# An RWKV-7 and block attention trunk: the state's carry over a chunk as a product and a sum beside PE, with another order of the work

## The chip, the cores and the metric

The kernel runs on one core of a Trainium2 chip. Its engines are TensorE (PE; its weight loads are shown apart as PEld), VectorE (DVE), ScalarE (ACT), GpSimd (POOL) and SyncE (SP), which issues most transfers. Each engine works off its own list of instructions in the order of that list, and semaphores hold an instruction back until what it reads is there. The metric is the device time of one execution in microseconds (us), lower being better.

## The reference

There are 256 tokens of width 1024 and two layers. The first is RWKV-7 time mixing with 16 heads of 64; the second is block attention with one block of 256 keys, so that it comes to causal attention behind the shared keys and values. Cut to what matters here, with the recurrence that the change touches:

```python
# layer 1
r, wdn, k, v, adn, gp = [(h + xx * mu[i]) @ w_in[:, cols(i)] for i in range(6)]
decay = exp(-exp(-softplus(-(w0 + tanh(wdn) @ w2)) - 0.5))
a = sigmoid(a0 + adn @ a2)
kk = normalized per head (k * k_k);  k = k * (1 + (a - 1) * k_a);  b = kk * a
def step(S, inp):                       # S: 64 x 64 for each head, over 256 tokens
    sa = einsum('bhvk,bhk->bhv', S, kk_t)
    S = S * d_t - sa[..., None] * b_t + v_t[..., None] * k_t
    y = einsum('bhvk,bhk->bhv', S, r_t)
y = (group_norm(y) + bonus) * silu(gp);  x = x + y @ w_out_a
# between: K and V from rms_norm(x) @ w_kv, K with QK-norm and partial rotary
# layer 2
q, g = rms_norm(x) @ w_in_b;  o = softmax(q K^T / 8, causal) V
x = x + (o * silu(g)) @ w_out_b
```

All inputs and outputs are float32.

## The kernel before

**Dense products.** The work is set by products of 256 by 1024 activations with weights, in two blocks of 128 tokens (b = 0, 1) and column halves of 512 (n = 0, 1). Most run as three reduced float32 products for one full one: ACT rounds a weight tile `raw` to `whi`, DVE forms the rest `wlo` (tiles of 128 by 1024), and the activations `z` are split in the same manner into `zhi` and `zlo`. PE then accumulates `wlo x zhi`, `whi x zlo` and `whi x zhi` into the banks `acc`. For the one matrix named in `WHOLE` ("v") the full float32 product `raw x z` is taken with no splitting. `dense` spawns such a product in four quarters of its contraction; `mixed_split` makes the mixed activations of layer 1.

**The recurrence.** It runs in chunks of 64 tokens, c = 0 to 3, for each half n of the heads (8 heads, in pairs on the two halves of the partitions, q = 0, 1). Within a chunk the 64 steps are solved at once by an inverse made beforehand (`inverse`, whose small products read and write ZX, AD, AB, QS and Z). `recurrence(n, c)` takes the state and values of the chunk, a tile UV of 64 + 64 rows, through these steps: `UV x WL` on PE; a copy of it by DVE into `u`; `u x Z` on PE; its negative, U, written back into UV by DVE and ACT; and for c < 3 `UV x NBK` on PE, which is what the chunk adds to the state. Two DVE operations (q = 0, 1) then write the sum times the decay `eLT` into the state part of the next chunk's UV. The old state has to be in that sum. For c = 0 it is zero; for c = 1 and 2 `chunk_y` copies it into the PSUM bank `st` by a product with the identity (`ident`, a part of the tile `con`), from which on `UV x NBK` accumulates:

```python
(mm(st[own[q]].rearrange("p j k -> p (j k)"), ident[own[q], own[q]],
    t[own[q], q].rearrange("p j k -> p (j k)"), 0.255, start=True, stop=False, skip_group_check=True)
 for q in range(2))
```

So the bank `st` is taken at the start of the chunk and given back behind the two DVE operations. `chunk_y` also makes the chunk's output with `UV x RR`; `group_norm` follows it on ACT, DVE and POOL.

**The order.** It isn't the order of the source. A planner (the class `Weave`) runs when the program is built: each piece of work is a generator that yields operations with estimated costs, waits for events or takes buffers; whenever an engine is free by these estimates, the ready operation of least number in `PR` goes next. `SWITCH` adds to that number where ACT would have to load another function table, `STICK` where PE would go from wide products to small ones or back, `ALT` says when an operation that DVE or POOL may do (`vg`) goes to POOL, and `KEEP` and `WARM` set when PE's clock is to be kept up (in the latter with products of a zero tile). `ORDER_A` and `ORDER_B` list the columns of the two layers' projections in the order in which their weights are fetched. Buffers are handed out in the same manner: five of `u` (`N_U2`), three of `raw`, four PSUM banks `ps`. The result is one fixed list for each engine.

**Lines.** In the rows a helper's line stands for all its uses: L413 for a product, L417 for a transposition by the identity, L308 for an operation of DVE, ACT or POOL. The tile's names tell them apart.

## Time and profile before

| what | us |
|---|---|
| median of 3 runs (356.96 to 357.12) | 356.97 |
| the profiled execution's own time | 358.23 |
| its span, from the first to the last instruction | 356.4 |
| PE busy | 348.1 (98%) |
| DVE busy | 290.6 (82%) |
| ACT busy | 205.7 (58%) |
| POOL busy | 47.0 (13%) |

A row's busy time counts an instruction from its start to its modelled end; on PE the ends overlap the next start, so what a product costs PE is read from one start to the next. Where a row ends in a bracket, it is the idle time of that engine just ahead of it, with the engine that ended it.

### The profile page before, as it was taken

How to read it: one execution, taken by the hardware profiler on the slowest of the kernel's cores; microseconds unless marked ns; L12 is line 12 of the kernel's file. 1: busy time of each engine (PE TensorE's matmuls, PEld its weight loads, DVE VectorE, ACT ScalarE, POOL GpSimd, SP SyncE). 2: the span in 40 equal slices, each digit the busy share in tenths (PEclk: the TensorE clock that was granted, in tenths of full speed). 3: DMA queues.
4: the chain of work that ended last, by engine and by line, in shares of the span. 5: the costliest groups of instructions: out<-in, count | busy, mean ns of one | idle time of the engine just before them, and what ended most of it. 6: DMA issues, size and time to landing. Idle time of an engine off the chain costs nothing.

```text
span 356.4 us, 7161 instructions
## 1 busy us (share of the span) xinstructions
PE 348.1 (98%) x2782; PEld 273.0 (77%) x2782; DVE 290.6 (82%) x582; ACT 205.7 (58%) x405; POOL 47.0 (13%) x71
## 2 busy tenths in 40 slices
PE   6999999999899999999999999999999999999995
PEld 6995877878458786567777788898877788789884
DVE  1899799999998988996669989885679969697723
ACT  3519988762336573254846547556459964696620
POOL 1100032000130000201001261060504004000000
PEclk9999999999999999999999999999999999999999
DMA  7825463763173741245545431365550366313403
GB/s 219 231 53 190 136 204 122 211 166 106 26 252 119 181 127 28 80 139 175 208 140 181 155 124 64 133 224 200 177 205 4 120 243 221 128 60 121 157 21 118
DMA packets 29738, 51.40 MB, mean 144 GB/s; under 512 B 4412, under 2 KB 5764, under 8 KB 29704
## 3 DMA queue, kind: packets, MB, share of 16 engines
q1 hardware_dynamic: 29480, 50.85, 44.8%
q8 instruction: 22, 0.36, 0.4%
q10 hardware_dynamic: 224, 0.09, 0.1%
q14 instruction: 12, 0.10, 0.1%
HBM read 48.32 MB, written 1.05 MB: 139 GB/s over the span
## 4 chain that ended last, share of the span: by engine, by line
PE 91%; DVE 5%; DMA 1%; issue 1%; ACT 1%; ACTq 0%; DVEq 0%
PE acc L413 63%; PE ps L413 21%; PE ps L417 7%; DMA con<-in_consts_dram 1%; DVE zlo L308 1%; DVE u L308 1%; DVE WL L308 1%; DVE RR L308 1%; DVE wlo L308 0%; DVE XF L308 0%; DVE xw L308 0%; ACTq L495 0%; DVE AD L308 0%; DVE eL L308 0%; ACT u L308 0%
## 5 line engine op out<-in xcount | busy, mean ns | idle before, releaser
L308 DVE TENSOR_TENSOR wlo<-raw,whi 128x1024 fp32r<-128x1024 f32 x70 | 85.0, 1218 | 26.7 <-ACT whi L308 26.2
L308 ACT ACTIVATE whi<-raw 128x1024 fp32r<-128x1024 f32 x70 | 73.9, 1060 | 40.7 <-PE acc L413 20.0
L413 PE MATMUL acc<-wlo,zhi 128*128 128x512 f32 x120 | 51.2, 427 | 0.0
L413 PE MATMUL acc<-whi,zhi 128*128 128x512 f32 x120 | 47.1, 392 | 0.0
L413 PE MATMUL acc<-whi,zlo 128*128 128x512 f32 x120 | 47.0, 391 | 0.0
L413 PE MATMUL acc<-whi,z 128*128 128x512 f32 x128 | 39.8, 392 | 0.0
L413 PEld LDWEIGHTS acc<-whi,z 128*128 128x128 f32 x128 | 24.1, 188 | 4.8
L413 PEld LDWEIGHTS acc<-wlo,zhi 128*128 128x128 f32 x120 | 22.5, 188 | 6.0 <-issue 0.5
L413 PEld LDWEIGHTS acc<-whi,zhi 128*128 128x128 f32 x120 | 22.5, 188 | 5.1
L413 PE MATMUL acc<-wlo,z 128*128 128x512 f32 x64 | 26.3, 410 | 0.0
L413 PEld LDWEIGHTS acc<-whi,zlo 128*128 128x128 f32 x120 | 22.6, 188 | 4.1 <-issue 0.5
L413 PE MATMUL acc<-zb,whi 128*128 128x256 f32 x128 | 23.3, 282 | 0.0
L413 PE MATMUL acc<-whi,zb 128*128 128x512 f32 x64 | 20.1, 395 | 0.0
L413 PE MATMUL acc<-whi,zf 128*128 128x512 f32 x64 | 19.8, 390 | 0.0
L413 PEld LDWEIGHTS acc<-zb,whi 128*128 128x128 f32 x128 | 19.7, 189 | 0.1
L413 PE MATMUL acc<-zb,wlo 128*128 128x256 f32 x64 | 18.8, 294 | 0.0
L308 POOL TENSOR_TENSOR nrm<-nrm,half 128x8 f32<-128x8 f32 x4 | 8.7, 2174 | 76.3 <-DVE nrm L308 76.3
L308 ACT ACTIVATE zhi<-u 128x256 fp32r<-128x256 f32 (+1 forms) x16 | 7.9, 522 | 17.1 <-DVE u L308 13.2
L413 PE MATMUL acc<-raw,zhi 128*128 128x512 f32 x32 | 15.5, 612 | 1.5 <-ACT u L308 1.5
L413 PE MATMUL acc<-raw,zlo 128*128 128x512 f32 x32 | 16.3, 615 | 0.0
L308 POOL TENSOR_SCALAR vr<-vr 128x8 f32<-128x8 f32 x4 | 3.0, 756 | 91.8 <-DVE vr L308 91.8
L308 ACT ACTIVATE AB<-ps 32x256 f32<-32x256 f32 (+1 forms) x32 | 10.3, 321 | 7.1 <-PE ps L413 5.9
(219 smaller groups left out, 749.2 us busy)
## 6 DMA issues: line engine op xcount, KB each, us to landing
raw<-in_w_in_a_dram SPq DMA_DIRECT2D x32, 512.0 KB, 4.6
raw<-in_w_kv_dram SPq DMA_DIRECT2D x16, 512.0 KB, 4.1
raw<-in_w_in_b_dram SPq DMA_DIRECT2D x16, 512.0 KB, 3.6
raw<-in_w_out_a_dram SPq DMA_DIRECT2D x8, 512.0 KB, 3.7
raw<-in_w_out_b_dram SPq DMA_DIRECT2D x8, 512.0 KB, 3.4
x<-in_x_dram SPq DMA_DIRECT2D x8, 256.0 KB, 3.4
out_dram<-x SPq DMA_DIRECT2D x8, 128.0 KB, 1.9
NBK<-kkh SPq DMA_DIRECT2D x6, 128.0 KB, 6.0
```

Source lines behind the costliest of these rows:

```text
L308: op = Op(eng, us, lambda: getattr(obj, name)(*a, **k), table=table, banks=banks(*a, *k.values()), port=port(eng, name, us, a, k))
L413: return us, lambda: nc.tensor.matmul(dst, l, r, **kw), size(r) * (1 if l.dtype == F32R else 4) * min(l.shape[0], size(l)) / P, banks(dst) ...
L417: return max(0.045, 0.1085 * src.shape[0] / P), lambda: nc.tensor.transpose(dst, src, idt), 256 * src.shape[0] / P, banks(dst), src.shape[ ...
```

## The change

**The carry.** The product with the identity is gone from `chunk_y`. For c = 1 and 2 a new part `old_state` multiplies the old state in UV by `eLT` into a buffer `u` (two operations, q = 0, 1, each of 64 partitions by 256). It has to be done before U is written into UV (`yield decayed`). `UV x NBK` now starts its bank afresh, the two operations that scale it stay as they were, and two more add the kept product to the next chunk's UV. Both pairs go through `vg`, so each may be planned on DVE or POOL; in the order that comes out all sixteen are on DVE. The bank is taken just ahead of `UV x NBK`, and one of the five buffers `u` is held from the product to the sum.

**The order.** `PR` and eight other numbers of the planner, `FIRST` and `ORDER_B` are replaced: in layer 2 the gate columns g0 and g1 now come last. `HALF` is empty and changes nothing.

```diff
-    def dense(label, zget, wap, col, evac, gates, order=None, used=None, whole=False):
+    def dense(label, zget, wap, col, evac, gates, order=None, used=None, whole=0):
...
-        ids = [quarter(wap, kq, col, whole=whole) for kq in range(4)]
+        ids = [quarter(wap, kq, col, whole=kq < whole) for kq in range(4)]
...
-        if c < 3:
-            pst = yield bank
-            st = j3(pst)
         pw_ = yield bank
         pw = j3(pw_)
         begun, early, carry = Event(), Event(), Event()
-        spawn(chunk_y(n, c, st if 0 < c < 3 else None, begun, early, carry), FOLLOW)
+        spawn(chunk_y(n, c, begun, early, carry), FOLLOW)
+        decayed = spawn(old_state(n, c), PR[f"rec{n}"]) if 0 < c < 3 else None
         yield at_start(pe(*(mm(pw[own[q], j, :], wl_[own[1 - q] if c == 0 else slice(0, 128), q, j, :],
                                t[own[1 - q] if c == 0 else slice(0, 128), q, j, :], 0.067, start=True, stop=True) for j, q in jq)), begun)
         ws_ = yield u2
@@ -1261,6 +1258,8 @@
                    for j, q in jq))
         u2.give(ws_)
         yield early
+        if decayed:
+            yield decayed
         yield [V.tensor_scalar(t[0:64, 0], pu[0:64], -1.0, None, op0=ALU.mult),
                S.activation(t[64:128, 1], pu[64:128], AF.Copy, scale=-1.0)]
         bank.give(pu_)
@@ -1268,13 +1267,27 @@
         if c == 3:
             weave.fire(carry)
             return
-        yield at_start(pe(*(mm(st[own[q], j, :], NBK[n, c][:, j, q, :], t[:, q, j, :], 0.067, start=(c == 0), stop=True,
-                               skip_group_check=True) for j, q in jq)), carry)
+        pst = yield bank
+        st = j3(pst)
+        yield at_start(pe(*(mm(st[own[q], j, :], NBK[n, c][:, j, q, :], t[:, q, j, :], 0.067, start=True, stop=True) for j, q in jq)), carry)
         yield event(f"v{n}{c + 1}")
         yield event(f"eLT{n}{b}")
         yield [V.tensor_tensor(uv[n, c + 1][own[q], q], st[own[q]],
                                eLT[n][own[q], :, c].unsqueeze(2).to_broadcast([64, 4, 64]), op=ALU.mult) for q in range(2)]
         bank.give(pst)
+        if decayed:
+            yield [vg("tensor_tensor", uv[n, c + 1][own[q], q], uv[n, c + 1][own[q], q], kept[n, c][own[q]], op=ALU.add) for q in range(2)]
+            u2.give(olds[n, c])
+
+    olds, kept = {}, {}
+
+    def old_state(n, c):
+
+        t = olds[n, c] = yield u2
+        kept[n, c] = t[:, 0:256].rearrange("p (j k) -> p j k", k=64)
+        yield event(f"eLT{n}{c // 2}")
+        yield [vg("tensor_tensor", kept[n, c][q * 64:q * 64 + 64], uv[n, c][q * 64:q * 64 + 64, q],
+                  eLT[n][q * 64:q * 64 + 64, :, c].unsqueeze(2).to_broadcast([64, 4, 64]), op=ALU.mult) for q in range(2)]
...
-    def chunk_y(n, c, st, begun, early, carry):
+    def chunk_y(n, c, begun, early, carry):
 
 
         b, cc = divmod(c, 2)
@@ -1299,11 +1312,7 @@
         yield begun
         if c > 0:
             yield pe(*(mm(py[own[q], j, :], wl_[own[q], 2, j, :], t[own[q], q, j, :], 0.067, start=(j == 0), stop=False,
-                          skip_group_check=True) for j, q in jq),
-                     *(() if st is None else
-                       (mm(st[own[q]].rearrange("p j k -> p (j k)"), ident[own[q], own[q]],
-                           t[own[q], q].rearrange("p j k -> p (j k)"), 0.255, start=True, stop=False, skip_group_check=True)
-                        for q in range(2))))
+                          skip_group_check=True) for j, q in jq))
...
-LAT, SWITCH, ALT = 0.16, 53.1, 69.22
+LAT, SWITCH, ALT = 0.16, 60.5, 81.22
...
-PR = {"x": 26.1, "wl": -1.1, "raw0": 32.4, "raw1": 29.1, "raw2": 43.5, "raw3": 13.7, "raw4": 20.1, "lora": -85.9,
+PR = {"x": 10.5, "wl": 12.4, "raw0": 58.4, "raw1": 22.7, "raw2": 63.8, "raw3": 33.7, "raw4": -1.3, "lora": 98,
...
-FIRST = [(0, 0), (0, 1), (1, 0), (1, 1), (2, 1), (2, 0), (3, 0), (3, 1)]
+FIRST = [(0, 0), (1, 0), (2, 0), (0, 1), (1, 1), (3, 0), (2, 1), (3, 1)]
-ORDER_B = ("k0", "g0", "q0", "k1", "v0", "q1", "v1", "g1")
+HALF = ""
+ORDER_B = ("k0", "q0", "k1", "v0", "q1", "v1", "g0", "g1")
-COLD, WINDOW, KEEP, WARM = 1.9, 3.4133, 994, (1.1, 20.94)
+COLD, WINDOW, KEEP, WARM = 1.9, 3.4133, 1189, (1.1, 16.51)
-SWAP, STICK = 0.1, 46.7
+SWAP, STICK = 0.1, 61.6
-LEAST, SPARE = 4, -8.64
+LEAST, SPARE = 4, -8.79
```

By engine, the two lists differ in number so: PE has 8 products fewer (`UV x con`), DVE 16 operations more, ACT two table loads more (8 for 6); POOL and SP have as many as before. The 35 products of the zero tile at the start stay 35.

In the order, PE goes through chunk c = 1 of the first half like this before (u is the copy of `UV x WL`, and the rows that read raw or wlo and whi are dense products):

```order
L413 MATMUL ps_348_1620<-UV_1241,WL_649 64x64 x8
L413 MATMUL ps_349_1624<-UV_1241,WL_649 64x64 x8
L413 MATMUL ps_347_1619<-UV_1241,con_71 64x256 x2
L413 MATMUL ps_352_1649<-u_351_1637,Z_1144 64x64 x8
L413 MATMUL acc_340_1566<-raw_323_1411,zhi_847 128x512 x2
L413 MATMUL ps_347_1619<-UV_1241,NBK_854 64x64 x8
L413 MATMUL ps_349_1624<-UV_1241,RR_812 64x64 x8
L413 MATMUL acc_341_1567<-raw_323_1411,zhi_847 128x512
L413 MATMUL ps_355_1695<-UV_1242,WL_651 64x64 x8
```


and now:

```order
L413 MATMUL ps_343_1600<-UV_1394,WL_626 64x64 x8
L413 MATMUL ps_344_1601<-UV_1394,WL_626 64x64 x8
L413 MATMUL acc_307_1392<-wlo_1435,zhi_1007 128x512
L413 MATMUL acc_307_1392<-whi_1434,zlo_1008 128x512
L413 MATMUL acc_307_1392<-whi_1434,zhi_1007 128x512
L413 MATMUL ps_347_1630<-u_346_1620,Z_1152 64x64 x8
L413 MATMUL acc_348_1638<-raw_314_1402,zhi_853 128x512 x2
L413 MATMUL acc_349_1639<-raw_314_1402,zhi_853 128x512
L413 MATMUL ps_352_1660<-UV_1394,NBK_846 64x64 x8
L413 MATMUL ps_344_1601<-UV_1394,RR_804 64x64 x8
L413 MATMUL acc_349_1639<-raw_314_1402,zhi_853 128x512
```

The identity product stood between `UV x WL` and `u x Z`; three dense products stand there now.

DVE's list where the sum of chunk c = 1 of the first half is carried on, before:

```order
L308 TENSOR_TENSOR tmp_1549<-xw_1551 128x72
L308 TENSOR_REDUCE xw_1551<-tmp_1549 128x2x6
L308 TENSOR_TENSOR tmp_1549<-xw_1551 128x98
L308 TENSOR_TENSOR UV_1242<-ps_347_1619,eLT_354 64x256 x2
L308 TENSOR_REDUCE xw_1551<-tmp_1549 128x2x7
L308 TENSOR_TENSOR tmp_1549<-xw_1551 128x512
L308 COPY u_358_1710<-ps_355_1695 128x256
L308 TENSOR_REDUCE XF_1550<-tmp_1549 128x64
L308 TENSOR_REDUCE vr_1721<-u_357_1700 128x8
```

and now:

```order
L308 TENSOR_TENSOR UV_1395<-ps_352_1660,eLT_355 64x256 x2
L308 TENSOR_SCALAR XF_1540<-xw_1541,con_71 128x16x16
L308 TENSOR_TENSOR yn_1592<-yn_1592,sg_1640 128x512
L308 STREAM_TRANSPOSE ZX_1715<-XF_1540 128x16x2x16
L308 TENSOR_TENSOR yn_1592<-yn_1592,vr_1693 128x512
L308 STREAM_TRANSPOSE ZX_1715<-ZX_1715 128x512
L308 TENSOR_TENSOR yn_1592<-yn_1592,vn_1397 128x512
L308 TENSOR_SCALAR Z_1728<-ZX_1715,con_71 128x16x32 x2
L308 TENSOR_TENSOR UV_1395<-UV_1395,u_345_1602 64x256 x2
L308 TENSOR_TENSOR wlo_1468<-raw_357_1703,whi_1467 128x1024
L308 TENSOR_TENSOR u_366_1770<-UV_1395,eLT_355 64x256 x2
L308 COPY u_371_1790<-ps_365_1769 128x256
```

The two scaled halves are followed seven rows later by the two sums, and these, behind one `wlo`, by the product for the next chunk; rows of the inverse and of `group_norm` stand between.

ACT's list where the first half's decay is made (eL, enL, sw), before:

```order
L308 ACTIVATE zhi_299<-u_107_376 128x512
L308 ACT_TABLE_LOAD
L308 ACTIVATE sw_358<-ps_129_442 128x512
L308 ACTIVATE eL_439<-ps_128_441 128x512
L308 ACTIVATE enL_440<-ps_128_441 128x512
L308 ACTIVATE whi_423<-raw_86_326 128x1024
L308 ACTIVATE whi_463<-raw_136_466 128x1024
L308 ACTIVATE sw_365<-ps_141_495 128x512
```

and now:

```order
L308 ACTIVATE ia_368<-ps_124_448 128x512
L308 ACTIVATE whi_468<-raw_108_369 128x1024
L308 ACTIVATE u_137_481<-sw_365 128x512
L308 ACT_TABLE_LOAD
L308 ACTIVATE sw_359<-ps_131_466 128x512
L308 ACTIVATE eL_450<-ps_130_465 128x512
L308 ACTIVATE enL_451<-ps_130_465 128x512
L308 ACTIVATE whi_504<-raw_112_412 128x1024
L308 ACTIVATE whi_516<-raw_134_474 128x1024
```

The rounding of the weights that the next `wlo` on DVE needs (whi_423 before, whi_468 now) stood behind the table load and three more operations; now it stands ahead of the load.

DVE's list where the first layer's output x is made and turned for the second (x, u, z), before:

```order
L308 COPY u_462_2403<-u_462_2403 128x2x64
L308 TENSOR_TENSOR zb_2519<-u_478_2508,zb_2518 128x4x128
L308 TENSOR_TENSOR u_494_2568<-ps_489_2551,vT_84 128x512
L308 COPY gT_97<-ps_493_2565 128x2
L308 TENSOR_TENSOR wlo_2560<-raw_465_2412,whi_2559 128x1024
L308 TENSOR_TENSOR u_497_2577<-ps_489_2551,vT_84 128x512
L308 TENSOR_TENSOR x_2041<-acc_446_2260,x_2041 128x512
L308 TENSOR_TENSOR z_2576<-u_494_2568,z_2575 128x512
L308 TENSOR_TENSOR wlo_2585<-raw_468_2434,whi_2584 128x1024
L308 TENSOR_TENSOR u_505_2612<-ps_503_2603,vT_84 128x512
L308 TENSOR_TENSOR rs_93<-ssq_95 128x1
```

and now:

```order
L308 TENSOR_TENSOR zb_2527<-u_481_2504,zb_2526 128x4x128
L308 TENSOR_TENSOR u_501_2588<-ps_493_2564,vT_84 128x512
L308 TENSOR_TENSOR x_2287<-acc_448_2263,x_2287 128x512
L308 TENSOR_TENSOR z_2587<-u_497_2575,z_2586 128x512
L308 TENSOR_TENSOR wlo_2570<-raw_473_2468,whi_2569 128x1024
L308 TENSOR_TENSOR u_508_2621<-ps_506_2612,vT_84 128x512
L308 TENSOR_TENSOR wlo_2593<-raw_478_2495,whi_2592 128x1024
L308 TENSOR_TENSOR u_512_2633<-ps_506_2612,vT_84 128x512
L308 TENSOR_TENSOR z_2632<-u_508_2621,z_2631 128x512
L308 TENSOR_TENSOR rs_93<-ssq_95 128x1
```

In both lists these rows lead to `rs`, the scale of the second block's rows. The last carry of the recurrence stands at row 313 of DVE's list before and at row 323 now.

## Rows read from the trace of the kernel before

**Rows 1.** The profile's page of the kernel before: busy time of each engine with its share of the span, the busy tenths in 40 slices for PE and DVE, and the chain of work that ended last by engine.

```profile
PE 348.1 (98%) x2782; PEld 273.0 (77%) x2782; DVE 290.6 (82%) x582; ACT 205.7 (58%) x405; POOL 47.0 (13%) x71
...
PE   6999999999899999999999999999999999999995
...
DVE  1899799999998988996669989885679969697723
...
PE 91%; DVE 5%; DMA 1%; issue 1%; ACT 1%; ACTq 0%; DVEq 0%
```

**Rows 2.** Busy time by stretch, one row a stretch (columns: stretch; its length; busy time of PE with its instructions, then PEld, DVE, ACT, POOL; the granted TensorE clock, 1.00 being its upper level; DMA share; GB/s).

```profile
0.00:41.00 41.00, 38.11 (x209) 31.92 (x210) 31.03 (x67) 22.71 (x45) 2.55 (x13) 1.00 0.56 163
41.00:84.00 43.00, 42.93 (x268) 33.64 (x267) 40.09 (x71) 32.27 (x74) 5.43 (x4) 1.00 0.60 176
84.00:112.00 28.00, 26.48 (x168) 16.59 (x167) 27.97 (x67) 10.85 (x26) 4.04 (x4) 1.00 0.34 104
112.00:160.00 48.00, 48.00 (x693) 34.49 (x690) 43.13 (x93) 24.18 (x55) 2.70 (x3) 1.00 0.42 121
160.00:192.00 32.00, 32.00 (x465) 24.22 (x464) 22.77 (x37) 19.69 (x33) 3.95 (x4) 1.00 0.49 164
192.00:208.00 16.00, 16.00 (x151) 12.25 (x150) 15.26 (x23) 7.25 (x11) 4.95 (x7) 1.00 0.58 194
```

**Rows 3.** The timeline of PE in the recurrence of the first half (columns: start, time, engine, line, operation, out<-in, xcount; neighbours of one form share a row, and the pitch is read from one start to the next).

```profile
132.17 0.39 PE L413 MATMUL acc<-whi,zhi 128*128 128x512 f32 x1
132.49 0.68 PE L413 MATMUL ps<-UV,WL 64*64 64x64 f32 x16
133.10 0.50 PE L413 MATMUL acc<-wlo,zhi 128*128 128x512 f32 x1
133.44 0.39 PE L413 MATMUL acc<-whi,zlo 128*128 128x512 f32 x1
...
138.07 0.69 PE L413 MATMUL ps<-UV,NBK 128*64 128x64 f32 x16
138.59 0.64 PE L413 MATMUL ps<-UV,RR 128*64 128x64 f32 x16
...
141.34 0.60 PE L413 MATMUL ps<-UV,con 64*64 64x256 f32 x4
141.77 0.63 PE L413 MATMUL ps<-u,Z 64*64 64x64 f32 x16
...
147.51 0.60 PE L413 MATMUL ps<-UV,con 64*64 64x256 f32 x4
147.95 0.63 PE L413 MATMUL ps<-u,Z 64*64 64x64 f32 x16
...
152.56 1.30 PE L413 MATMUL ps<-UV,WL 128*64 128x64 f32 x32
```

**Rows 4.** The timeline of PE in the recurrence of the second half.

```profile
180.88 0.60 PE L413 MATMUL ps<-UV,con 64*64 64x256 f32 x4
181.32 0.63 PE L413 MATMUL ps<-u,Z 64*64 64x64 f32 x16
...
187.94 0.60 PE L413 MATMUL ps<-UV,con 64*64 64x256 f32 x4
188.38 0.63 PE L413 MATMUL ps<-u,Z 64*64 64x64 f32 x16
```

**Rows 5.** The timeline of DVE in the recurrence of the first half.

```profile
138.80 0.86 DVE L308 TENSOR_TENSOR UV<-ps,eLT 64x256 f32<-64x256 f32 x2
...
141.18 0.42 DVE L308 COPY u<-ps 128x256 f32<-128x256 f32 x1
...
151.38 0.86 DVE L308 TENSOR_TENSOR UV<-ps,eLT 64x256 f32<-64x256 f32 x2
```

**Rows 6.** Groups of DVE's instructions, different shapes apart (line, engine, operation, out<-in, shapes, count; busy time, mean ns of one; idle time before them and what ended it).

```profile
L308 DVE TENSOR_TENSOR wlo<-raw,whi 128x1024 fp32r<-128x1024 f32 x70 | 85.0, 1218 | 26.7 <-ACT whi L308 26.2
...
L308 DVE TENSOR_TENSOR UV<-ps,eLT 64x256 f32<-64x256 f32 x12 | 5.0, 419 | 0.9 <-PE ps L413 0.7
```

**Rows 7.** The timeline of DVE where operations of 256 columns that read and write SBUF alone follow one another.

```profile
105.67 0.41 DVE L308 TENSOR_TENSOR kkh<-ia,enL 128x256 f32<-128x256 f32 x1
106.01 0.41 DVE L308 TENSOR_TENSOR ia<-ia,enL 128x256 f32<-128x256 f32 x1
```

**Rows 8.** The timeline of DVE around the idle time after 40 us; the last bracket is the idle time ahead of a row and what ended it.

```profile
40.09 0.68 DVE L308 TENSOR_TENSOR zlo<-u,zhi 128x512 fp32r<-128x512 f32 x1
43.02 1.23 DVE L308 TENSOR_TENSOR wlo<-raw,whi 128x1024 fp32r<-128x1024 f32 x1 [2.25 <-ACT whi L308]
```

**Rows 9.** The timeline of ACT at the same place.

```profile
39.18 1.28 ACT L308 ACT_TABLE_LOAD   x1
...
41.92 1.07 ACT L308 ACTIVATE whi<-raw 128x1024 fp32r<-128x1024 f32 x1
```

**Rows 10.** The timeline of PE around its longest wait behind the start.

```profile
90.98 0.39 PE L413 MATMUL acc<-whi,zhi 128*128 128x512 f32 x1
92.89 3.27 PE L413 MATMUL acc<-raw,zhi 128*128 128x512 f32 x7 [1.52 <-ACT u L308]
```

**Rows 11.** The timeline of DVE and, in the next group, of ACT at that wait.

```profile
91.46 0.69 DVE L308 TENSOR_TENSOR eL<-acc,eL 128x512 f32<-128x512 f32 x1
```

**Rows 12.** The timeline of ACT at that wait.

```profile
92.24 0.60 ACT L308 ACTIVATE u<-acc 128x512 f32<-128x512 f32 x1 [0.86 <-DVE eL L308]
```

More of the change, by code (lines that the diff above doesn't have):

```diff
@@ L786, in mixed_split @@
         halves = places_of[key] = []
-        if key in WHOLE:
+        whole = []
+        if key in WHOLE + HALF:
             halves.append((yield zs))
-            whole = [t.bitcast(F32) for t in halves[0]]
-            zmix[key] = lambda b: lambda part, kt: whole[kt // 4][:, kt % 4, b * P:(b + 1) * P]
-        else:
-            zmix[key] = lambda b: lambda part, kt: halves[kt // 4][part][:, kt % 4, b * P:(b + 1) * P]
+            whole = [t.bitcast(F32) for t in halves[0]][0:1 if key in HALF else 2]
+        zmix[key] = lambda b: lambda part, kt: (whole[kt // 4] if part is None else halves[kt // 4][part])[:, kt % 4, b * P:(b + 1) * P]
         def piece(q, ts):
             n = ts.stop - ts.start
-            if key in WHOLE:
+            if q // 2 < len(whole):
                 z = whole[q // 2][:, q % 2 * 2:q % 2 * 2 + 2, ts]
@@ L805, in piece @@
                                              hT[kt // 4][:, kt % 4, t1], op0=ALU.mult, op1=ALU.add)
-            if key not in WHOLE:
+            if q // 2 >= len(whole):
                 yield from split(z, *(t[:, q % 2 * 2:q % 2 * 2 + 2, ts] for t in halves[q // 2]))
@@ L823, in mixed_split @@
             for q in range(4):
-                if q % 2 == 0 and key not in WHOLE:
+                if q % 2 == 0 and q // 2 >= len(halves) and key not in WHOLE:
                     halves.append((yield zs))
@@ L1396, in yoco @@
         dense(label, zmix_of(key), w_in_a[0], col, {"k": evac_k, "r": evac_r, "v": evac_v, "g": evac_g}[key](n),
-              [[f"z{key}{b}{q}" for q in range(4)] for b in range(NB)], order=FIRST if i == 0 else None, used=used(key), whole=key in WHOLE)
+              [[f"z{key}{b}{q}" for q in range(4)] for b in range(NB)], order=FIRST if i == 0 else None, used=used(key), whole=4 if key in WHOLE else 2 if key in HALF else 0)
     x1 = {}
@@ L1693, in yoco @@
     weave.run()
[L1697 removed]
+LAT, SWITCH, ALT = 0.16, 60.5, 81.22
 OWN = {"PE": 0.0, "V": 0.13, "S": 0.115, "G": 0.096, "D": 0.0}
[L1700 removed]
[6 rows of a table removed]
[L1707 removed]
+PR = {"x": 10.5, "wl": 12.4, "raw0": 58.4, "raw1": 22.7, "raw2": 63.8, "raw3": 33.7, "raw4": -1.3, "lora": 98,
[6 rows of a table added]
+      "values": 97.4, "out": -14.8}
 ORDER_A = ("k0", "r0", "k1", "r1", "v0", "g0", "v1", "g1")
[L1710 removed]
+FIRST = [(0, 0), (1, 0), (2, 0), (0, 1), (1, 1), (3, 0), (2, 1), (3, 1)]
 FIRST_B = [(0, 0), (1, 0), (2, 0), (3, 0), (0, 1), (1, 1), (2, 1), (3, 1)]
```

1 line of the change is left out of this document (removed), and 12 rows, old and new, of the table PR.

## The prediction

> **What bounds the kernel now.** The page comes first: PE is busy for 348.1 of 356.4 us, and 91% of the chain that ended last is PE's, 5% DVE's [rows 1]. So the time is PE's work plus PE's waits, and DVE (82%) matters only where it makes PE wait. The view by stretch says where that can be. From 112 to 208 us PE is busy without a gap, and DVE is idle for 4.87 us until 160, 9.23 until 192 and 0.74 until 208, 14.84 in all; from 84 to 112 it is the other way round, DVE busy for 27.97 of 28 us and PE short of 1.52 [rows 2]. The granted clock is 1.00 in all of them, the upper level. That one wait of PE's, 1.52 us ahead of 92.89, ends with ACT's `u<-acc`, and that with DVE's `eL<-acc,eL` at 91.46 [rows 10 to 12]: a bank is freed late because DVE is late.
>
> All terms below are changes of the profiled execution's own time, 358.23 us. The median is 1.26 us under that (356.97), and I take the same off at the end. Where I speak of work ahead of an instruction, I went through an engine's list and gave each row the mean pitch of its form in the trace; the differences of such sums are what I use, not their absolute level.
>
> **What is removed.** Four chunks lose the identity product, each `x4` in the trace. From its start to that of `u x Z` it takes 0.43 and 0.44 us in the first half [rows 3] and 0.44 and 0.44 in the second [rows 4]. PE waits for nothing there, so this is path: **-1.75 us**. But the product also filled a wait: DVE copies `UV x WL` into `u` from 141.18 on, 0.42 us, and `u x Z` starts at 141.77 [rows 3, 5]. Now three dense products stand in that place, so nothing is exposed if their weights are there; what it costs is one more change between wide and small products. Such a change is 0.32 us for a pitch that is 0.23 within the dense run (132.17 to 132.49), and 0.34 for the first dense product behind the small ones (133.10 to 133.44) [rows 3]: some 0.2 us for both. In the two lists dense runs are broken by small float32 groups 43 times before and 42 times now, by transpositions 38 and 36 times: the new order saves elsewhere what it spends here, **-0.3 us**. PE's work ahead of the first dense product is 0.2 us more: **+0.2**.
>
> **What is added.** Sixteen operations of 64x256 on DVE, none on POOL. The nearest row with PSUM as a source is `UV<-ps,eLT`, 419 ns [rows 6]; operations of 256 columns from SBUF to SBUF follow one another at 0.34 us (105.67 to 106.01) [rows 7]. So 5.4 to 6.7 us on DVE; I take 0.38 each, between the two, **6.1 us**, since the halves of 64 partitions run in pairs of 0.86 for two [rows 5]. Two table loads on ACT, 1.28 us each [rows 9], are covered by ACT's 42% of idle time, or cost 2.6 us if both stood on the path. Longer hold of one `u` buffer, shorter hold of a bank: their effect is in the order already, and I give them no term of their own (0, with bounds of one such wait, -0.5 to +0.5).
>
> [...]
>
> **Where the 6.1 us lie.** All of them fall between 118 and 171 us of DVE's work, so in the stretch from 112 to 192 where DVE idles 14.1 us [rows 2]. On the carry itself they lengthen the chain: DVE's scaling ends at 152.24 and the next `UV x WL` starts at 152.56 [rows 3, 5], 0.32 us behind. Now the sum (two operations, 0.76) comes in between. In the new list PE has three to nine more dense products around each step, and the work that PE has ahead of each `UV x WL` exceeds DVE's ahead of the sum by 3 us or more beyond what the two engines stand apart: I take **0** here, with a bound of 3.4 (below).
>
> **The wait at 91 us.** DVE's lateness has a source: it is idle for 2.25 us ahead of 43.02, waiting for ACT's `whi` [rows 8], and ACT rounds that tile at 41.92 only because a table load of 1.28 us at 39.18 and three operations go first [rows 9]. In the new list that rounding stands ahead of the load, and the next one is wanted by DVE 8.7 us of work later. So DVE should be 2.25 us earlier, less 0.6 us of work more ahead of the `eL` row, less 0.4 for the later start of the first dense products: 1.25. PE's work ahead of its wait is equal (81.97 us in both). The 1.52 us become about 0.3: **-1.2 us**; bounds 0 (the idle time only moves) and -1.5.
>
> **The turn of x into layer 2.** Here the new order gives something back. Behind the last carry DVE has much to do: `wlo`, x, u, z. Before, that carry's row on DVE waits for a product that ends when PE has done 10.6 us more of its work than DVE of its own, and the `wlo` and `rs` rows that PE wants soon after have a margin of 12.7: PE doesn't wait. With 6 us more on DVE and the dense products drawn forward, the two become 5.06 and 4.28 now. To 5.06 come 0.21 us from the end of the product at 138.59 to DVE at 138.80, and 0.32 from DVE's end to PE [rows 3, 5]; the excess over 4.28 is **+1.3 us** of waiting, at `wlo`, `rs` or both. Bounds: 0, if each row runs a little faster than its mean; and +3, if DVE also waits for `whi` there as it does elsewhere.
>
> **Layer 2.** Gates come last; the softmax of the last heads has 5.7 us of dense products beside it, where it had 6.0, and the last product, sum and transfer are the same. **0**.
>
> **Sum:** -1.75 - 0.3 + 0.2 + 0 - 1.2 + 1.3 = -1.75. 358.23 - 1.75 = 356.5 for a profiled execution, and **355.2 us** as the median (-0.5%). What decides the sign is the 1.75 of PE's work that is gone; the two terms of the order nearly cancel.
>
> **Rivals.**
> - *DVE is in time at the turn to layer 2.* Its margins hold, because 14.1 us of idle time take up 6.1 without delay. For it: PE has no gap from 112 to 208 [rows 2]. Against it: most of that idle time is spent waiting for PE's products, and cannot be used later. Then the +1.3 falls away: 353.9.
> - *The wait at 91 stays.* ACT loads a table somewhere else ahead, or DVE waits for another `whi`; the idle time moves. Then the -1.2 falls away and the kernel gains -0.55: 356.4, within 0.2%, which is about what a measurement of this kernel can tell from no change.
> - *Slower: the sum on DVE's list.* DVE takes its rows in order; the sum stands seven rows behind the scaling in one chunk, and whatever PE waits for behind it waits too. If each of the four steps is exposed for the sum, at the 0.86 us of a pair whose source is PSUM [rows 5], it costs 3.4 us: 355.2 + 3.4 = 358.6. From 0.6 us a step on, the kernel is slower than before by more than 0.2%. For it: only 0.32 us between DVE and PE at 152.56 [rows 3, 5], and a list fixed by estimates. Against it: dense products stand between in the new list.
> - That the change doesn't do what it says (sums on POOL, products still there) is excluded by the lists.
>
> **How the numbers follow.** The forecast has 0.42, with 354.6 to 356.1 as its own range; in time at the turn 0.17 (353.9); the wait stays 0.20 (356.4); slower 0.21 (358.6). Faster by over 0.2% (below 356.26): the first two, 0.59. Within 0.2%: 0.20. Slower (above 357.68): 0.21. For 8 times in 10 the range goes down to 353.6, a little under the first rival, and up to 358.3, which leaves out the dearer part of the slow one.
>
> **What would show it.** In the profile of the changed kernel: no `ps<-UV,con`, and PE's busy time about 1.8 us lower; DVE's 5.4 to 6.7 higher; no idle time of 2 us on DVE near 43; PE's wait near 91 at 0.3 us or gone; no PE waits in the recurrence for a row `UV<-UV,u`; and a wait of PE of 1 to 2 us near 205 to 222 on `wlo` or `rs`. The forecast is wrong if PE shows waits for `UV` between 125 and 190, if the wait at 91 is as long as before, or if new waits appear in layer 2, where I found no reason for one.

## The result, and the profile after

| kernel | median, us | runs | ratio to before, 95% interval |
|---|---|---|---|
| before | 357.05 | 4 (356.96 to 357.48) | |
| changed | 359.45 | 4 (359.33 to 360.2) | 1.0069 (1.0052 to 1.0087) |

The change is 0.7% slower, 2.4 us. The profiled execution of the changed kernel took 359.55 us (span 357.8), 1.3 us more than that of before (358.23); the second profile of before below shows that such single executions differ by 0.9 us in the start alone, so the ratio is what counts. Of one kernel below (`e1_carry_only`) two of six executions, 368.18 and 368.81 us, lie over 1.5% above its fastest and are left out of its median and ratio.

The page of the changed kernel, the rows that answer to [rows 1], and PE's granted clock:

```profile
PE 347.8 (97%) x2766; PEld 271.6 (76%) x2766; DVE 297.7 (83%) x598; ACT 207.3 (58%) x407; POOL 49.3 (14%) x71
...
PE   5999999999799999999999999999999999999995
...
DVE  1999989899997899998699989887898786878623
...
PEclk9999999999899999999999999999999999999999
...
PE 79%; DVE 14%; DMA 2%; POOL 2%; issue 1%; ACT 1%; SPq 1%; DVEq 0%; POOLq 0%; ACTq 0%
```

PE is busy for as long as before although it has eight products less, and one slice of the clock, the eleventh, is not full. The view by stretch, with the stretches of [rows 2] and the next:

```profile
0.00:41.00 41.00, 37.37 (x211) 30.91 (x212) 32.22 (x68) 23.48 (x45) 2.89 (x13) 1.00 0.62 184
41.00:84.00 43.00, 43.00 (x270) 33.97 (x269) 39.82 (x74) 31.98 (x74) 4.37 (x4) 1.00 0.54 156
84.00:112.00 28.00, 26.10 (x206) 16.79 (x205) 25.43 (x61) 9.29 (x21) 4.36 (x4) 0.94 0.34 104
112.00:160.00 48.00, 48.00 (x556) 31.97 (x555) 45.10 (x95) 24.52 (x54) 1.87 (x2) 1.00 0.43 128
160.00:192.00 32.00, 32.00 (x552) 25.25 (x551) 26.61 (x51) 20.48 (x37) 3.90 (x4) 1.00 0.47 150
192.00:208.00 16.00, 16.00 (x151) 12.85 (x148) 14.31 (x23) 6.20 (x10) 3.06 (x2) 1.00 0.37 107
208.00:226.00 18.00, 17.48 (x86) 13.27 (x85) 18.00 (x31) 11.00 (x21) 6.03 (x17) 1.00 0.45 153
```

The last stretch was this before:

```profile
208.00:226.00 18.00, 18.00 (x91) 14.76 (x90) 16.50 (x30) 10.67 (x20) 4.23 (x14) 1.00 0.26 89
```

The recurrence (112 to 208) is as full on PE as before. Three stretches are not: 0 to 41, 84 to 112 with a clock of 0.94, and 208 to 226. The second first, on PE's timeline, against [rows 10]:

```profile
90.06 0.39 PE L413 MATMUL acc<-whi,zhi 128*128 128x512 f32 x1
92.35 3.66 PE L413 MATMUL acc<-raw,zhi 128*128 128x512 f32 x4 [1.90 <-ACT u L308]
```

The wait at 91 us has not shrunk from 1.52 us; it is 1.90. And the four records behind it take 3.66 us. The view by 2 us (the clock is the third number from the end) says why:

```profile
90.00:92.00 2.00, 0.45 (x2) 0.03 (x1) 2.00 (x7) 0.44 (x2) 0.00 (x0) 1.00 0.02 7
92.00:94.00 2.00, 1.65 (x2) 0.72 (x3) 2.00 (x7) 0.89 (x3) 0.00 (x0) 0.63 0.00 0
94.00:96.00 2.00, 2.00 (x4) 0.87 (x3) 2.00 (x6) 0.57 (x1) 1.01 (x1) 0.52 0.00 0
96.00:98.00 2.00, 2.00 (x6) 0.82 (x5) 2.00 (x4) 0.00 (x0) 0.63 (x1) 1.00 0.00 0
```

After PE stood still, it ran at the lower level from about 92.5 us, just behind its next start, until about 96 us (0.63 and 0.52 are means of two levels: by half microseconds the clock reads 1.00 from 92.0 to 92.5, 0.50 from 93.0 to 95.5 and 1.00 from 96.0 on): four records from 94 to 96 us, where six are done from 96 to 98 at 1.00. So in this profile the lower clock follows the wait; group 2 has profiles that kept the clock behind the same wait, and the wait at this place in the kernel before, 1.52 us, left the clock at 1.00.

DVE's timeline at the two places of [rows 8] and [rows 11]:

```profile
43.80 0.69 DVE L308 TENSOR_TENSOR kkh<-acc,bv 128x512 f32<-128x512 f32 x1 [0.74 <-PE acc L413]
...
46.18 0.69 DVE L308 TENSOR_REDUCE nrm<-u 128x8 f32<-128x512 f32 x1 [1.09 <-ACT u L308]
...
90.92 0.69 DVE L308 TENSOR_TENSOR eL<-acc,eL 128x512 f32<-128x512 f32 x1
```

The idle time of 2.25 us is gone, but 0.74 and 1.09 have come in its place. Counted from the first dense product (24.72 before, 24.66 now), DVE reaches `eL` 0.48 us earlier (66.74 and 66.26), and PE reaches its last product ahead of the wait 0.86 us earlier (66.26 and 65.40). So the wait grew by the difference, 0.38.

The new operations, shapes apart, and the carry of chunk 1 of the first half on DVE's timeline:

```profile
L308 DVE TENSOR_TENSOR UV<-UV,u 64x256 f32<-64x256 f32 x8 | 3.3, 417 | 0.2
L308 DVE TENSOR_TENSOR u<-UV,eLT 64x256 f32<-64x256 f32 x8 | 3.3, 416 | 0.2
```

```profile
149.47 0.86 DVE L308 TENSOR_TENSOR UV<-ps,eLT 64x256 f32<-64x256 f32 x2
...
154.67 0.87 DVE L308 TENSOR_TENSOR UV<-UV,u 64x256 f32<-64x256 f32 x2
```

The sum comes 5.2 us behind the scaling, and PE waits for neither. At the turn to layer 2 it does wait, for `zlo`, by 0.52 us in the bracket (two starts, 211.18 and 212.19, are 1.01 apart where 0.23 is usual, so 0.78 in all):

```profile
211.18 0.50 PE L413 MATMUL acc<-zlo,zhi 128*128 128x512 f32 x1
212.19 0.50 PE L413 MATMUL acc<-zhi,zlo 128*128 128x512 f32 x1 [0.52 <-DVE zlo L308]
```

### The profile page after: what moved, and what is told of

Same layout as the page of the kernel before. It is cut to its first block, busy times and chain, and to the rows that moved or that the text cites. A ratio compares the mean times of both kernels' runs of the same rounds, so it can differ in the third digit from the quotient of the medians.

```text
span 357.8 us, 7154 instructions
## 1 busy us (share of the span) xinstructions
PE 347.8 (97%) x2766; PEld 271.6 (76%) x2766; DVE 297.7 (83%) x598; ACT 207.3 (58%) x407; POOL 49.3 (14%) x71
## 4 chain that ended last, share of the span: by engine, by line
PE 79%; DVE 14%; DMA 2%; POOL 2%; issue 1%; ACT 1%; SPq 1%; DVEq 0%; POOLq 0%; ACTq 0%
PE acc L413 54%; PE ps L413 18%; PE ps L417 6%; DVE u L308 2%; DVE zlo L308 2%; DVE wlo L308 2%; DMA x<-in_x_dram 1%; DVE vn L308 1%; POOL vr L308 1%; DMA raw<-in_w_kv_dram 1%; POOL rs L308 1%; DVE WL L308 1%; DVE RR L308 1%; DVE x L308 1%; DVE UV L308 1%
## 5 line engine op out<-in xcount | busy, mean ns | idle before, releaser
L413 PE MATMUL acc<-wlo,zhi 128*128 128x512 f32 x120 | 52.4, 437 | 0.0
L413 PE MATMUL acc<-whi,zlo 128*128 128x512 f32 x120 | 47.0, 392 | 0.0
L413 PE MATMUL acc<-whi,zhi 128*128 128x512 f32 x120 | 47.0, 392 | 0.0
L413 PE MATMUL acc<-whi,z 128*128 128x512 f32 x128 | 39.8, 392 | 0.0
L413 PEld LDWEIGHTS acc<-whi,z 128*128 128x128 f32 x128 | 24.1, 188 | 4.9
L413 PEld LDWEIGHTS acc<-wlo,zhi 128*128 128x128 f32 x120 | 22.5, 187 | 6.6 <-issue 0.7
L413 PEld LDWEIGHTS acc<-whi,zhi 128*128 128x128 f32 x120 | 22.5, 188 | 5.1
L413 PE MATMUL acc<-wlo,z 128*128 128x512 f32 x64 | 26.2, 410 | 0.0
L413 PEld LDWEIGHTS acc<-whi,zlo 128*128 128x128 f32 x120 | 22.6, 188 | 4.2 <-issue 1.0
L413 PE MATMUL acc<-zb,whi 128*128 128x256 f32 x128 | 23.3, 282 | 0.0
L413 PE MATMUL acc<-whi,zb 128*128 128x512 f32 x64 | 20.0, 394 | 0.0
L413 PE MATMUL acc<-whi,zf 128*128 128x512 f32 x64 | 19.8, 390 | 0.0
L413 PEld LDWEIGHTS acc<-zb,whi 128*128 128x128 f32 x128 | 19.7, 189 | 0.0
L413 PE MATMUL acc<-zb,wlo 128*128 128x256 f32 x64 | 18.8, 295 | 0.0
L308 POOL TENSOR_TENSOR nrm<-nrm,half 128x8 f32<-128x8 f32 x4 | 7.9, 1974 | 77.7 <-DVE nrm L308 77.7
L413 PE MATMUL acc<-raw,zhi 128*128 128x512 f32 x32 | 16.2, 661 | 1.9 <-ACT u L308 1.9
L413 PE MATMUL acc<-raw,zlo 128*128 128x512 f32 x32 | 15.2, 602 | 0.0
L413 PEld LDWEIGHTS acc<-wlo,z 128*128 128x128 f32 x64 | 12.1, 189 | 3.3 <-issue 0.6
```

The lines of the kernel that those rows point to most:

```text
L308: op = Op(eng, us, lambda: getattr(obj, name)(*a, **k), table=table, banks=banks(*a, *k.values()), port=port(eng, name, us, a, k))
L413: return us, lambda: nc.tensor.matmul(dst, l, r, **kw), size(r) * (1 if l.dtype == F32R else 4) * min(l.shape[0], size(l)) / P, banks(dst) ...
```

## The experiments

Each run has its own median of before on the same chip (357.5, 356.8, 357.4 and 357.3 us in the four groups); the ratios are to that. Where a kernel's lists are said to be another's row for row, this was read from the lists. Where an edit shifts the lines, L421 and L425 stand for L413 and L417.

**Group 1: which half of the change loses the time, and does the clock matter?** `e1_before` is the kernel before again. `e1_carry_only` is the new code with the old numbers, `e1_order_only` the old code with the new numbers; up to the recurrence, each has the same list as the kernel that its numbers come from. `e1_fill` adds this to the changed kernel, with a cost of nearly nothing so that the planner moves nothing:

```diff
             done = [0] * 4
+            if label == "v0":
+                yield event(f"w{ids[0]}")
+                yield event(gates[0][0])
+                fb = yield bank
+                fill = pe(*(mm(fb[:, 0:P], ident, ident, 1e-6, start=True, stop=True) for _ in range(10)))
+                fill.columns, fill.count = 0.0, 0
+                yield fill
+                bank.give(fb)
```

> The kernel before, unchanged, for a second profile beside the others. Its profiled execution was 358.2 us where its median is 357.0; the changed one's profile and median agree (359.55, 359.45). If the first profile was dearer than usual at one place, the difference of the two kernels is 2.4 us and not 1.3, and this profile shows that place: 357.0, with the wait of PE near 91 us shorter than 1.5 us. If profiles of this kernel are always 1.2 us above its other runs, it shows 358.2 again.

> The new carry with the old numbers of the planner; the lists are those of before up to the recurrence (PE row 403, DVE row 225). Theory 1 (the carry is sound, the new order loses it all): PE loses 1.75 us of work and nothing waits, so 355.2 to 356.2. Rival (the sums on DVE make PE wait): 357.5 to 359.5, with PE or the copy of UV x WL waiting behind UV<-UV,u.

> The old carry with the new numbers of the planner; the lists are those of the changed kernel up to the recurrence (PE row 391). Theory 1: all of the loss is here, 1.75 us more than the changed kernel, 360.8 to 361.5, with the clock at its lower level for some 3.4 us behind the wait at 90 us. Rival: the loss comes with the carry, so 356.5 to 357.5.

> The changed kernel with ten products of the identity with itself (2.2 us of PE, into a free bank, read by nobody) in the wait at 90 us, all lists else the same. Theory 1a (the clock falls because PE stands still there, and this costs 1.7 us): granted clock 1.00 all through and 357.6 to 358.0. Rival (the clock falls there for another reason, or the lower level costs nothing because PE is waiting for DVE in that stretch): clock or time as in the changed kernel, 359.2 to 359.7.

| run | median | ratio to before |
|---|---|---|
| e1_before | 357.02 | 0.9989 (0.9963 to 1.0015) |
| e1_carry_only (four executions) | 362.83 | 1.0161 (1.0117 to 1.0205) |
| e1_order_only | 366.73 | 1.0257 (1.0225 to 1.0288) |
| e1_fill | 358.79 | 1.0039 (1.0022 to 1.0057) |

Neither half is good alone: the new carry costs 1.6% under the old numbers (its executions spread over 361 to 366 us), the new numbers cost 2.6% with the old carry, and both together 0.7%. My first theory (the carry sound, the loss all in the order) falls with `e1_carry_only`. PE's timeline of it shows waits at the end of the recurrence:

```profile
198.18 1.30 PE L413 MATMUL ps<-UV,WL 128*64 128x64 f32 x32
200.44 0.68 PE L413 MATMUL ps<-u,Z 64*64 64x64 f32 x16 [0.96 <-DVE u L308]
202.87 1.08 PE L417 MATMUL ps<-con,yn 128*128 128x128 f32 x4 [1.75 <-DVE yn L308]
```

PE has nothing left to do beside the last chunk, waits 0.96 and 1.75 us, and the clock falls again (0.85 and 0.72 in the stretches 200 to 204 and 204 to 208).

`e1_order_only` missed its theory too: it was expected at 360.8 to 361.5 with a lower clock behind 90 us, and took 366.73 with the clock at 1.00 there, behind the same wait of 1.90 us. It loses at the turn into layer 2, where PE is busy for 14.75 of the 18 us from 208 to 226 (clock 0.91), above all here:

```profile
213.40 0.66 PE L417 MATMUL ps<-con,x 128*128 128x128 f32 x4 [1.72 <-DVE x L308]
```

`e1_fill` holds the clock, as the first of its theories said, though not the time that went with it (357.6 to 358.0; 358.79 came). Its PE timeline and two stretches:

```profile
91.12 0.40 PE L413 MATMUL acc<-whi,zhi 128*128 128x512 f32 x1
91.36 2.40 PE L413 MATMUL ps<-con 128*128 128x128 f32 x20
93.59 3.60 PE L413 MATMUL acc<-raw,zhi 128*128 128x512 f32 x8
```

```profile
92.00:94.00 2.00, 2.00 (x17) 1.78 (x16) 2.00 (x6) 1.12 (x2) 0.00 (x0) 1.00 0.00 0
94.00:96.00 2.00, 2.00 (x6) 0.95 (x5) 2.00 (x8) 0.63 (x1) 0.00 (x0) 1.00 0.00 0
```

Eight records of `raw x zhi` now take 3.60 us, where four took 3.66. The kernel is still 0.4% slower than before, so the clock is not all.

`e1_before` shows the spread of the start: its first dense product begins at 23.83 us instead of 24.72, and its runs go from 355.6 to 359.5. Its wait at 91 is 1.52 us again, so that is not where its first profile was dear.

**Group 2: what the products and the sums are worth by themselves, and the start.** `e2_after` is the changed kernel again. In `e2_nosum` and `e2_noid` the planner counts the operations as ever, but they are not written into the program, so both leave the old state out of the carry. This is cut from `e2_nosum`; `e2_noid` does the like to the eight products of the kernel before:

```diff
+        mute = lambda op: (setattr(op, "emit", lambda: None), setattr(op.alt, "emit", lambda: None), op)[2]
-        yield [vg("tensor_tensor", kept[n, c] ...
+        yield [mute(vg("tensor_tensor", kept[n, c] ...
-            yield [vg("tensor_tensor", uv[n, c + 1] ...
+            yield [mute(vg("tensor_tensor", uv[n, c + 1] ...
```

In `e2_start` two transfers (x of the second block) are held back on SP's queue until those of wl have been issued.

> The changed kernel again, for comparison on the same chip as the next three: 2.0 to 2.6 us above the kernel before.

> The changed kernel without the sixteen new operations of DVE (the old state is left out of the carry for c = 1 and 2, so the recurrence forgets it); all lists else the same row for row. The prediction's reading (DVE has room for them in the recurrence, and only the turn into layer 2 waits): 0.5 to 1.3 us faster than the changed kernel, by that wait. Rival (the sums lengthen the carry, PE waits for them): 2 us or more faster, up to 3.4. Third (they cost nothing): within 0.3 us.

> The kernel before without the eight identity products (the old state is left out of the carry for c = 1 and 2), all lists else the same row for row. If they are PE's path, as the prediction counts them: 1.75 us faster than before, 355.3. Rival (they filled the time of DVE's copy of UV x WL, 0.42 us each, and PE now stands still there): 0 to 0.5 us faster, with PE waiting for u in all four chunks.

> The changed kernel with the transfers of x for the second block issued behind those of wl, as before, instead of ahead of them; all other lists the same row for row. Theory (these 0.5 MB delay the constants with the identity, for which PE's first transposition waits 0.7 us longer than before): 0.5 to 0.8 us faster than the changed kernel, with PE's first transposition at 6.3 us again instead of 7.0. Rival (other transfers delay it as well, or the start is made up before the first dense product): within 0.3 us.

| run | median | ratio to before |
|---|---|---|
| e2_after | 359.24 | 1.0071 (1.0047 to 1.0095) |
| e2_nosum | 359.35 | 1.0076 (1.0048 to 1.0103) |
| e2_noid | 355.76 | 0.9978 (0.9956 to 1.0001) |
| e2_start | 359.7 | 1.009 (1.0061 to 1.012) |

The sixteen new operations cost nothing: without them the changed kernel takes the same time (the profiles agree more closely than the medians can: from the first dense product to the last product 328.83 us without, 328.89 with). That settles the rival of the slow sum, in this list, against it. PE's wait for `zlo` at the turn to layer 2 is there without them as well:

```profile
212.40 0.50 PE L413 MATMUL acc<-zhi,zlo 128*128 128x512 f32 x1 [0.53 <-DVE zlo L308]
```

The eight products, taken out of the old list, are worth less than the 1.75 us that they take there: 0.8 us by the ratio (0 to 1.6). In `e2_noid`, PE now waits for the copy of `UV x WL`, as the prediction's remark on the filler has it. One chunk of before, and two of `e2_noid`:

```profile
140.21 1.30 PE L413 MATMUL ps<-UV,WL 128*64 128x64 f32 x32
141.34 0.60 PE L413 MATMUL ps<-UV,con 64*64 64x256 f32 x4
141.77 0.63 PE L413 MATMUL ps<-u,Z 64*64 64x64 f32 x16
```

```profile
137.46 1.30 PE L413 MATMUL ps<-UV,WL 128*64 128x64 f32 x32
138.92 0.68 PE L413 MATMUL ps<-u,Z 64*64 64x64 f32 x16 [0.16 <-DVE u L308]
...
143.58 1.30 PE L413 MATMUL ps<-UV,WL 128*64 128x64 f32 x32
145.06 0.68 PE L413 MATMUL ps<-u,Z 64*64 64x64 f32 x16 [0.18 <-DVE u L308]
```

From `UV x WL` to `u x Z` the four chunks take 0.10, 0.09, 0.17 and 0.36 us less than before, 0.7 in all. That is the old list, where nothing else stands in the gap; it doesn't say what the products were worth in the new one, where dense products stand there and PE shows no gap from 112 to 208.

`e2_start` missed: it made PE's first transposition later (7.83 us) instead of earlier. Its issue rows show wl's transfers out at 3.51 us, where the changed kernel has 4.92 and the kernel before 1.63; why the constants land later still is not shown. It shows something else: its wait at 91 us is as long (the pitch from the last product is 2.3 us, as in the changed kernel), but the clock stayed at 1.00, and from the first dense product to the last product it took 327.08 us where the changed kernel took 328.88. It is not alone in this. Of the seven profiles with the wait of 1.90 us and nothing put into it, three show the lower clock behind it (changed, `e2_after`, `e2_nosum`) and four do not (`e1_order_only`, `e2_start`, and of the groups below `e3_start` and `e4_startzeros`). The rows of `e1_order_only` and `e4_startzeros`, sixteen records in 7.13 us, where fourteen took 7.97 in the changed kernel:

```profile
92.24 7.13 PE L413 MATMUL acc<-raw,zhi 128*128 128x512 f32 x16 [1.90 <-ACT u L308]
```

```profile
92.82 7.13 PE L421 MATMUL acc<-raw,zhi 128*128 128x512 f32 x16 [1.90 <-ACT u L316]
```

**Group 3: the start with the issue order of before, the sums under the old numbers, and the banks of k1.** In `e3_start` wl's transfers are issued right behind x of the first block, as before, all other lists being those of the changed kernel; `e3_fillstart` adds eight products to the wait at 91; `e3_carry_nosum` is `e1_carry_only` without the sums; `e2_kfirst` changes one number:

```diff
-                spawn(evac(b, acc[b]), prio)
+                spawn(evac(b, acc[b]), -150 if label == "k1" else prio)
```

> The changed kernel with the transfers of wl issued right behind the first block's x, as in the kernel before; all other lists the same row for row. Theory (in the new issue order the constants with the identity land later, PE stands still for 2.4 to 2.7 us instead of 1.4 to 1.95, and in executions where the clock has risen early it falls again): PE's first transposition at 6.4 us or earlier, no lower clock before the first dense product, and 0.7 to 1.5 us faster than the changed kernel. Rival (the start isn't where the median is lost): within 0.4 us of the changed kernel, 2.4 us above before.

> The same, and eight products of the identity with itself in the wait at 90 us. If the start and the clock behind that wait are all that the change loses, it stands at or under the kernel before: 356.0 to 356.9, from the first dense product to the end 327.1 to 327.7 us (before 327.5 to 328.0). If something else loses time, it stays above 357.5.

> The new carry with the old numbers of the planner, without the sixteen operations of DVE (the old state is left out of the carry for c = 1 and 2); all lists else those of the run with the sums. If DVE's time in the sums is what made that run 5.8 us slower than before: 356 to 358. If the list that the planner makes around them is to blame, whatever DVE does in them: 362 to 365, with the same waits near 200 us.

> The changed kernel with the banks of the products k1 emptied by DVE ahead of other work (number -150 in the planner), so that the product behind the wait at 90 us finds free banks; the lists are the same until PE's row 300, DVE's 125 and ACT's 112. If that wait is one for DVE's order of work: the wait falls from 2.06 us to under 0.5 and the clock stays up there, 2 to 3.5 us faster than the changed kernel unless the list behind it has new waits. Rival (DVE is simply late by its work ahead): the wait moves to another row within 5 us of it.

| run | median | ratio to before |
|---|---|---|
| e3_start | 358.55 | 1.0041 (1.0022 to 1.006) |
| e3_fillstart | 358.11 | 1.0023 (1.0002 to 1.0043) |
| e3_carry_nosum | 363.2 | 1.0158 (1.0107 to 1.021) |
| e2_kfirst | 381.59 | 1.0678 (1.0644 to 1.0711) |

`e3_carry_nosum` is as slow as with the sums (1.0161), within the 0.5% of the two intervals: under the old numbers too it is the list, not DVE's time in the sums. The wait for `yn` is there without them:

```profile
207.85 0.63 PE L417 MATMUL ps<-con,yn 128*128 128x128 f32 x4 [1.75 <-DVE yn L308]
```

`e3_fillstart` was expected at 356.0 to 356.9 if start and clock were all, and stands at 358.11. `e2_kfirst` missed both of its theories: the planner, given the one number, puts a product of the inverse where PE waits for DVE's `ZX` by 17.4 us, and the clock is low until 114 us (its mean is 0.962 in that execution). It tells nothing of the wait at 91, and much of how far one number moves a list.

The start is a second place of the loss: with the old issue order the kernel gains 0.3% (1.0041 for 1.0071), though part of that can be the clock at 91 us, which held in its profile. PE's first transposition waits until 6.98 us in the changed kernel, and until 6.24 here. It reads the constants `con`, whose transfer took 5.2 us to land in the changed kernel and 4.4 us here and before (6.0 in `e2_start`); the first bracket names x, which came last by the profile:

```profile
6.98 0.32 PE L417 MATMUL ps<-con,vrow 56*128 56x56 f32 x1 [2.59 <-DMA x<-in_x_dram]
```

```profile
6.24 0.24 PE L425 MATMUL ps<-con,vrow 56*128 56x56 f32 x1 [1.85 <-DMA con<-in_consts_dram]
...
9.41 0.26 PE L425 MATMUL ps<-con,vrow 16*128 16x16 f32 x1 [1.29 <-DMA vrow<-in_norm_b_dram]
```

The last row shows what is left: in the new list nothing stands between PE and the second row of gains, where before 18 records of the zero tile (8.90 us in the profile of before) and others lay ahead of it. In this execution the clock, already up at the first transposition (the eight that follow it take 1.09 us, where they take 1.97 in the profile of before), fell again:

```profile
7.00:10.00 3.00, 1.64 (x11) 1.25 (x10) 2.48 (x4) 0.42 (x1) 0.65 (x2) 0.72 0.77 237
10.00:13.00 3.00, 3.00 (x16) 3.00 (x16) 0.87 (x2) 0.95 (x4) 0.00 (x0) 0.50 0.87 320
```

and the first dense product began at 26.63 us. By the mean of 0.72 the fall came at about 8.3 us, only 0.2 us into the wait ahead of 9.41, so that wait is not shown to be its cause. In the new list, with nothing added at the start, the clock was up at the first transposition in five profiles and fell soon after in all five, behind waits for that transposition of 1.85 (`e3_start`), 2.14, 2.29, 2.36 and 2.61 us (`e2_kfirst`, `e1_order_only`, `e2_after`, `e2_nosum`; 0.58 from 7 to 10 us in `e2_after`); in the old list it was up so early in two, behind 1.41 and 1.68 us (`e2_noid`, `e1_carry_only`), and stayed (in `e2_noid` the 18 records of the zero tile behind the transpositions take 2.17 us, where they take 3.77 in the profile of before).

**Group 4: is that all?** `e4_startzeros` is `e3_start` with seven more products of the zero tile, three behind the seventh and four ahead of the gains; `e4_full` adds the eight products in the wait at 91; `e4_before_fill` puts these eight into the same wait of the kernel before.

> The changed kernel with wl's transfers early (as in e3_start) and seven more products of the zero tile in the start: three in PE's wait for the identity, four ahead of its wait for the second row of gains. All other lists the same row for row. Theory (of what e3_start still loses, the rest is the clock that rises early and falls again because PE stands still at 7.8 to 9.4 us): no lower clock before the first dense product when it has risen early, and 0.5 to 1 us faster than e3_start, so 0 to 0.6 us above before. Rival (the spread of the start is chance and the same in both kernels): as e3_start, 1.1 us above before.

> The same and eight products of the identity with itself in the wait at 90 us. If start and clock are all that the change lost, it is now under the kernel before by what its list is shorter from the first dense product on, 0.6 to 1.1 us: 356.3 to 356.9 where before has 357.4. If it stays at 358, as e3_fillstart did, something in the start is still open.

> The kernel before with the same eight products in its own wait of 1.5 to 1.7 us at 91 us. Its clock doesn't fall there in most executions, so it should gain little: within 0.4 us of before. If it gains 1 us or more, the filled wait is worth as much without the change, and a gain of the other run says nothing of the carry.

| run | median | ratio to before |
|---|---|---|
| e4_startzeros | 358.1 | 1.0013 (0.9993 to 1.0033) |
| e4_full | 357.07 | 1.0002 (0.9987 to 1.0017) |
| e4_before_fill | 357.32 | 1.0005 (0.9983 to 1.0026) |

With start and clock treated, all of the loss is gone, and no more than that: `e4_full` was expected 0.6 to 1.1 us under before and stands level with it. In its twelve executions the mean granted clock was 0.998 or more, where all ten of the changed kernel (its own four and `e2_after`) have 0.995 or less. Its profile takes 327.65 us from the first dense product to the last product, as much as before, where `e3_fillstart`, with the same lists behind the start, took 326.89; half of that is a new wait of 0.38 us for DVE's `u` at 291 us. Its stretch at the old wait:

```profile
84.00:112.00 28.00, 27.91 (x280) 19.28 (x280) 27.16 (x64) 10.50 (x25) 4.37 (x4) 1.00 0.36 105
```

`e4_startzeros` comes within 0.13% of before (its interval reaches it) with nothing put into the wait at 91 us. The kernel before gains nothing from the filled wait; its clock held there in all five profiles that have the wait of 1.52 us unfilled (for one, 1.00 in the profile of before, [rows 2]), and its mean clock is 0.997 or more in 22 of 29 executions. No kernel that I ran is faster than before beyond the measurement.

## Why the prediction was wrong

It gave 355.2 us, 353.6 to 358.3, and 359.45 came. From PE's start of the first dense product to that of its last product, read from the profiles, the parts separate:

| lists and state | profiles | us |
|---|---|---|
| list of before | before, e1_before, e4_before_fill | 327.48, 327.96, 327.57 |
| new list, clock held (wait at 91 left as it is) | e2_start, e3_start, e4_startzeros | 327.08, 327.01, 327.09 |
| new list, clock held by products in the wait | e1_fill, e3_fillstart, e4_full | 327.67, 326.89, 327.65 |
| new list, clock lower behind the wait | changed, e2_after, e2_nosum | 328.88, 328.89, 328.83 |

- **The step that failed is the wait at 91 us**, put at -1.2. It measured +0.4, and in the changed kernel's profiles 1.8 more for the clock behind it (328.87 less 327.06). DVE's idle time near 43 went as I said, but most of it came back within 4 us, at waits for PE and ACT, and I had not asked what is late next there: DVE reached `eL` 0.5 us earlier, where I had 1.25. PE, whose work I had counted as equal, came 0.86 us earlier, and so waited longer. And I priced a wait of PE at its own length, with no thought of the clock after it. The second rival (the wait stays) had the mechanism, at 356.4, without that price.
- **The start**, put at +0.2 by counting PE's work, is the second. The first dense product begins at 24.66, 24.29, 24.89, 24.61, 25.70 and 24.34 us in six profiles with the new start (changed, e2_after, e2_nosum, e1_order_only, e1_fill, e2_kfirst; mean 24.75) and at 24.72, 23.83, 23.98, 21.72, 22.00 and 24.82 with the old one (before, e1_before, e4_before_fill, e2_noid, e1_carry_only, e3_carry_nosum; mean 23.51): 1.2 us, an estimate from few profiles, of which the old ones lie 3 us apart. With products in the wait at 91 us in both, the treated start is worth 0.37% (`e1_fill` 1.0039, `e4_full` 1.0002), 1.3 us, of which 0.2 is the longer filling (2.47 us from the product ahead of it to the one behind, against 2.28). That the constants land later in the new issue order had no term in my sum.
- **The products removed**, -1.75: not refuted. `e2_noid` shows them worth about 0.7 in the old list, where they covered a wait; but in the new list dense products stand in that place, PE has no gap in the recurrence, and the sum below, with the full 1.75 in it, is 0.25 us from what was measured. No run puts the products back into the new list.
- **The sums on DVE**, 0: right, by `e2_nosum`, though they are dearer than I took them (0.42 us each, 6.6 in all, for 6.1). So the slow rival, 358.6, had the sign and not the cause.
- **The turn to layer 2**, +1.3: a wait in the stretch named, 0.8, but for `zlo` and not for `wlo` or `rs`, and as long without the sums (0.53 against 0.52). DVE's 6 us more, from which I had worked it out, do not make it; with them ruled out the new order is left, so the near size is luck.
- **Together**: -1.75 - 0.3 + 0.4 + 0.8 is -0.85 for the new list with its clock held (the -0.3 was not tested by itself); measured from the first dense product on, it is about -0.6 (327.06 against the mean of 327.67). With 1.8 for the clock and some 1.2 for the start it is the 2.4 us of the medians, closer than terms from so few profiles can be trusted. Nor do these two simply add up: in all three profiles with another start and nothing in the wait the clock held at 91 us.

What stays open: why the list planned around the new carry is 1.6% slower under the old numbers (shown is only that DVE's sums are not the reason), what the shorter hold of the PSUM bank brings by itself, which wasn't tried, and what decides whether a wait costs the clock: the same 1.90 us cost it in three profiles and not in four, and 1.52 us left it up in all five.

## What to carry to other kernels

A wait of the busiest engine was not worth its length alone (behind the 1.90 us here the lower clock cost 1.8 us more in three profiles of seven): look at the granted clock in the stretch behind it, and when a change moves such a wait, price the clock on both sides. When an operation is removed from a full engine, ask what it covered, and what covers that now; taken out alone, with all lists fixed (not written, while the planner still counts it), it shows its worth in that list and in no other. And where a planner makes the order, one number may move everything: compare kernels whose lists are the same row for row but for the thing in question.
